# The first stage of a YOCO-style decoder step (S5 layer beside memory keys and values) written as one fixed order of instructions

## The chip, the cores and the metric

One Trainium2 chip, one core. The metric is device time in microseconds (us) of one execution; less is better. The kernel is written in a tile framework: the code names tiles and instructions, the framework adds the semaphores between engines, and its scheduler decides in which order each engine's instructions stand in the program. Once built, each engine runs its own list strictly in that order.

## What is computed

A decoder trunk of two layers over 256 prompt tokens and 64 sample tokens (320 columns, width 1024). Layer 0 mixes with an S5 state space, layer 1 with latent attention; each layer then attends to 256 memory tokens and applies an MLP. The change concerns the S5 part of layer 0 and the keys and values of its memory:

```python
def s5_mixer(u, a_re, a_im, log_dt, b_re, b_im, c_re, c_im, d_skip, w_glu, h0_re, h0_im):
    ...
    _, _, h_re, h_im = lax.associative_scan(
        _complex_affine_combine, (a_seq_re, a_seq_im, bu_re, bu_im), axis=1)
    ...
    y = jnp.einsum('gkn,btgn->btgk', cr, h_re) - jnp.einsum('gkn,btgn->btgk', ci, h_im)
    y = y.reshape(bsz, t, dm) + d_skip.astype(f32) * u.astype(f32)
    g = jax.nn.gelu(y, approximate=False).astype(u.dtype)
    z = g @ w_glu
    out = z[..., :dm] * jax.nn.sigmoid(z[..., dm:])
    return out, h_re[:, -1], h_im[:, -1]

def mem_kv(mem, g, w_k, w_v):
    b, m, _ = mem.shape
    mn = rms_norm(mem, g)
    k = (mn @ w_k).reshape(b, m, MEM_HEADS, MEM_HEAD_DIM)
    v = (mn @ w_v).reshape(b, m, MEM_HEADS, MEM_HEAD_DIM)
    return k, v
```

## The kernel before

Engines are called PE (matmuls and transposes), ACT, DVE, POOL (GpSimd) and SP (which only starts DMAs here). ACT and POOL start DMAs too; a DMA that an engine starts stands in that engine's list.

**The first stage** is `s5_scan` (L711) with the generator `mem_kv` (L575), which makes the memory keys and values. Its parts, by the tiles that name them in the rows:

- Parameters: `an` and `ld` are loaded, turned by PE (`aps`, L768) into `AR`, and become powers PR and PI through exponentials and sines on ACT (L774 to L786) and small products on DVE.
- Memory: `mt` (256 memory tokens) is turned in eight blocks (`mps`) and copied with its gain to `mnp`, four blocks by ACT (L568) and four by DVE (L566). Sixteen chunks of w_mem_k and w_mem_v (512 KB each) are loaded into the weight buffers `wraw`, `whi`, `wlo`, two of each kind, in turn. A chunk gives eight products (`mm`, L600 for keys, L602 for values). Eight groups of two chunks are then written out.
- Tables b and c: `natb` and `natc` are turned in four steps each (`bcps`) and copied to `m_b` and `m_c` (L822).
- x: `xc` holds the tokens by chunk of eight. ACT sums its squares (`sq`, L835), scales it to `xr` (L942), PE turns it (`ups`), ACT copies it to `U` (L950).
- State side, four quarters (hq 0 to 3), `state_side` (L988): DVE makes `tq` from m_b (three products of 128x1024 per half), PE turns it (`rps`), ACT copies it to `rt` (L934), PE multiplies with U (`sps`, L996), ACT copies to `H`.
- Output side, four quarters, `out_side` (L1003): DVE makes `ca` and `ct` from m_c; PE makes the responses (`kps`, L1029, L1033), ACT copies them to `kk` (L1036), DVE adds the skip term (L1042), and eight DMAs on SP spread kk into the Toeplitz tile `tt` (L1045). There is one kk buffer, so a quarter's copies wait until the DMAs of the quarter before have read it.
- `scan` (L1049) runs on DVE twice, over two quarters each, and copies the result to `HS`; `outputs` (L1088) multiplies tt with U and ca, ct with HS on PE (`yps`), turns the result (`ytp`), and ACT applies the GELU and writes `xh`, DVE `xl` (L97, L98).

After that come the GLU products (`glu`, L691, through `dense`, L220): w_glu in sixteen chunks, each loaded by two DMAs into `wraw`, split by ACT into `whi` (L191) and by DVE into `wlo` (L192); three matmuls (L216 to L218) per block. The first group has four chunks and 96 matmuls; two of its chunks need only hq 0 and 1.

**What sets the order.** The scheduler orders each engine's list by its own estimate of times; `tc.issue_after(...)` ties single instructions. GLU loads, conversions and matmuls may so be placed between instructions of the first stage. The two halves of tt are cleared at the start by GpSimd:

```python
        for t in tts:
            nc.gpsimd.memset(t, 0.0)
```

DMAs that SP and ACT start share eight completion slots (DMAHW0 to DMAHW7), handed out in the order in which the code creates the DMAs, over both engines together. Before an engine starts a DMA, its list waits until the last DMA of the same slot has landed.

Of the kernel before, what the change touches and what calls it, by code (L numbers as in the profile page):

```python
# [10 lines left out]
F32 = mybir.dt.float32  # L11
# [74 lines left out]
EARLY = 4  # L86
# [3 lines left out]
class Trunk:  # L90
# [88 lines left out]
    def load_chunk(self, srcs, cols):  # L179

        nc = self.nc
        raw = self.wtile('raw', F32)
# [20 lines left out]
    def plain_tile(self):  # L203
        kind = ('raw', 'hi', 'lo')[self.plain % 3]
        self.plain += 1
        return self.wtile(kind, F32)
# [128 lines left out]
    def build(self):  # L335
        tc, nc, I, O = self.tc, self.nc, self.I, self.O
        with ExitStack() as ctx:
# [11 lines left out]
            self.fillers = []  # L349
# [50 lines left out]
    def mem_gains(self, pool):  # L400
        nc, cp = self.nc, self.cp
        self.gmT = cp.tile([128, 16], F32, name="gmT")
        gn = pool.tile([16, 128], F32, name="gmn")
        nc.scalar.dma_start(gn, self.I['mem_in_norm'].rearrange("l (j p) -> (l j) p", p=128))
        yield
        ps = self.ps_mm.tile([128, 512], F32, name="gps", tag="mm")
        self.transpose(ps[:, :16], gn)
        nc.vector.tensor_copy(self.gmT, ps[:, :16])
        yield

    def load_gains(self, pool):
# [7 lines left out]
        nc.sync.dma_start(gn[106:109, :], I['q_norm'].rearrange("l (j p) -> (l j) p", p=128))  # L419
        ps = self.ps_mm.tile([128, 512], F32, name="gps", tag="mm")  # L420
        self.transpose(ps[:, :109], gn)
        nc.vector.tensor_copy(self.gT[:, :109], ps[:, :109])
# [104 lines left out]
    def mem_x(self, pool, plain=False):  # L527
        if plain:
            return pool.tile([128, KD, MT], F32, name="mnp"), None
        return (pool.tile([128, KD, MT], F32R, name="mnh"), pool.tile([128, KD, MT], F32R, name="mnl"))  # L530
# [7 lines left out]
    def mem_root(self, sq):  # L538

        nc, mt = self.nc, self.mt  # L540
        rm = self.rm = self.cp.tile([128, 2, 2], F32, name="r_mem")
        for i in range(2):
            nc.scalar.activation(sq, mt[i], AF.Square, accum_out=rm[:, 0, i:i + 1])
        yield
        nc.scalar.activation(rm[:, 1], rm[:, 0], AF.Sqrt, bias=self.eps[:, 0:1], scale=1.0 / D)
        nc.vector.reciprocal(rm[:, 0], rm[:, 1])
        yield

    def mem_rows(self):
        nc = self.nc  # L550
        ps = self.ps_mm.tile([128, 512], F32, name="mrb", tag="mm")
        for i in range(2):
            self.transpose(ps[:, i * 128:(i + 1) * 128], self.rm[:, 0, i:i + 1].to_broadcast([128, 128]))
        nc.vector.tensor_copy(self.rB, ps[:, :MT])

    def mem_prepare(self, l, mp, x):
# [3 lines left out]
        for j in range(KD):  # L560
            ps = (self.ps_at if l else self.ps_mm).tile([128, 512], F32, name="mps", tag="at" if l else "mm")
# [3 lines left out]
            if xl is None and j % 2:  # L565
                nc.vector.tensor_scalar(xh[:, j, :], m, g(j), None, op0=ALU.mult)  # L566
            else:
                last = nc.scalar.activation(xh[:, j, :], m, AF.Copy, scale=g(j))  # L568
            if xl is not None:
                nc.vector.scalar_tensor_tensor(xl[:, j, :], m, g(j), xh[:, j, :].bitcast(F32),  # L570
                                               op0=ALU.mult, op1=ALU.subtract)
        self.kt = mp.tile([128, KD, MT], F32, name="kt", tag="kt")
        return last

    def mem_kv(self, l, op, x):  # L575
# [6 lines left out]
        done = {}  # L582

        def products(g):
            W, c0 = (Wk, g * 256) if g < 4 else (Wv, (g - 4) * 256)
            ps = [self.ps_mm.tile([128, 512], F32, name="mm", tag="mm") for _ in range(2)]
            for k0 in range(0, KD, 4):
                src = W[:, k0:k0 + 4, c0:c0 + 256]
                if xl is None:
                    raw = self.ahead.pop(0) if self.ahead else self.load_plain(src)  # L590
                    with ExitStack() as after:
                        if self.mem_hold is not None:
                            after.enter_context(self.tc.issue_after(self.mem_hold.ins))
                        for kk in range(4):
                            k = k0 + kk
                            for b in range(2):
                                w = raw[:, kk * 256:(kk + 1) * 256]
                                bs = slice(b * 128, (b + 1) * 128)
                                if g < 4:
                                    last = nc.tensor.matmul(ps[b][:, :MT], w[:, bs], xh[:, k, :], start=k == 0, stop=k == KD - 1)  # L600
                                else:
                                    last = nc.tensor.matmul(ps[b][:, :256], xh[:, k, bs], w, start=k == 0, stop=k == KD - 1)  # L602
                    if g < EARLY and k0 == 0:
                        yield last
                    continue
                hi, lo = self.load_chunk([(lambda t: t.rearrange("p (k c) -> p k c", c=256), src)], 1024)
                for kk in range(4):
                    k = k0 + kk
                    for b in range(2):
# [3 lines left out]
                        else:  # L613
                            s = slice(kk * 256, (kk + 1) * 256)
                            ms = slice(b * 128, (b + 1) * 128)
                            self.mm3(ps[b][:, :256], xh[:, k, ms], xl[:, k, ms], hi[:, s], lo[:, s], k == 0, k == KD - 1)
            if g < 4:
                for b in range(2):
                    nc.scalar.activation(kt[:, 2 * g + b, :], ps[b][:, :MT], AF.Copy)
            done[g] = ps  # L620
            if not l and g < EARLY:
                yield last

        if not l:
            for g in range(EARLY):
                yield from products(g)
# [1279 lines left out]
```

## Time and profile before

| what | us |
|---|---|
| median of 3 runs | 1213.37 |
| runs | 1212.70, 1213.37, 1215.11 |
| the profiled execution, own time | 1214.59 |
| its span, first to last instruction | 1212.9 |
| PE busy in the span | 1134.4 (94%) |
| DVE, ACT, POOL busy | 701.8, 558.1, 54.2 |

The rows read from the trace stand further down. In a timeline row the first number is the start in us from the span's start, the second the time from the first start to the last end, `xN` the number of instruction records (a product has two records, a transpose one), and the bracket the idle time ahead of it with what ended it. A row of DMA on SPq or ACTq is the starting of the DMA, not its transfer.

### The profile page before, as it was taken

How to read it: one execution, taken by the hardware profiler on the slowest of the kernel's cores; microseconds unless marked ns; L12 is line 12 of the kernel's file. 1: busy time of each engine (PE TensorE's matmuls, PEld its weight loads, DVE VectorE, ACT ScalarE, POOL GpSimd, SP SyncE). 2: the span in 40 equal slices, each digit the busy share in tenths (PEclk: the TensorE clock that was granted, in tenths of full speed). 3: DMA queues.
4: the chain of work that ended last, by engine and by line, in shares of the span. 5: the costliest groups of instructions: out<-in, count | busy, mean ns of one | idle time of the engine just before them, and what ended most of it. 6: DMA issues, size and time to landing. Idle time of an engine off the chain costs nothing.

```text
span 1212.9 us, 21264 instructions
## 1 busy us (share of the span) xinstructions
PE 1134.4 (94%) x8233; PEld 1027.4 (85%) x8233; DVE 701.8 (58%) x1344; ACT 558.1 (46%) x1012; POOL 54.2 (4%) x91
## 2 busy tenths in 40 slices
PE   5799789899899999999999999999998999999995
PEld 4688679886699999999988984579966899999995
DVE  6697834674369643564686674417842675335553
ACT  5664554444355543553464362224443465334531
POOL 1000000000000000000000154100000000000001
PEclk9799899999899999999999999989999999999998
DMA  9346358747244544444453555447470434444541
GB/s 179 98 132 153 81 130 290 261 154 262 88 123 132 170 154 147 148 156 144 159 149 109 154 178 157 141 146 283 147 269 25 138 122 141 156 139 144 167 142 44
DMA packets 155233, 185.37 MB, mean 153 GB/s; under 512 B 20847, under 2 KB 123516, under 8 KB 155068
## 3 DMA queue, kind: packets, MB, share of 16 engines
q1 hardware_dynamic: 145660, 175.36, 47.0%
q10 hardware_dynamic: 7008, 5.47, 1.4%
q0 software_dynamic: 2464, 3.19, 0.9%
q8 instruction: 65, 1.06, 0.4%
q14 instruction: 36, 0.29, 0.1%
HBM read 175.41 MB, written 6.21 MB: 150 GB/s over the span
## 4 chain that ended last, share of the span: by engine, by line
PE 75%; ACT 3%; DVE 3%; issue 1%; DMA 0%; POOLq 0%; POOL 0%; ACTq 0%; DVEq 0%
PE mm L217 19%; PE mm L216 19%; PE mm L218 19%; PE kt L103 2%; PE sps L1282 2%; PE s L1765 2%; PE ops L1297 1%; ACT whi L191 1%; PE pov L1339 1%; PE s L1806 1%; PE ltp L103 1%; DVE wlo L192 1%; PE pps L1317 1%; PE turn L103 1%; PE s L1768 1%
## 5 line engine op out<-in xcount | busy, mean ns | idle before, releaser
L192 DVE TENSOR_TENSOR wlo<-wraw,whi 128x1024 fp32r<-128x1024 f32 (+1 forms) x216 | 259.6, 1205 | 280.4 <-ACT whi L191 262.2
L191 ACT ACTIVATE whi<-wraw 128x1024 fp32r<-128x1024 f32 (+1 forms) x216 | 224.6, 1045 | 304.8 <-PE mm L217 253.3
L217 PE MATMUL mm<-xl,whi 128*128 128x320 f32 x944 | 292.8, 313 | 1.6 <-DVE xl L293 0.9
L216 PE MATMUL mm<-xh,whi 128*128 128x320 f32 x944 | 278.9, 316 | 15.7 <-ACT whi L191 4.6
L218 PE MATMUL mm<-xh,wlo 128*128 128x320 f32 x944 | 282.2, 312 | 0.0
L216 PEld LDWEIGHTS mm<-xh,whi 128*128 128x128 f32 x944 | 174.9, 191 | 19.6 <-ACT xh L1309 5.0
L217 PEld LDWEIGHTS mm<-xl,whi 128*128 128x128 f32 x944 | 179.7, 190 | 3.2 <-DVE xl L293 1.7
L218 PEld LDWEIGHTS mm<-xh,wlo 128*128 128x128 f32 x944 | 176.9, 190 | 0.2 <-DVE wlo L192 0.2
L216 PE MATMUL mm<-hh,whi 128*128 128x320 f32 x512 | 158.0, 309 | 0.0
L217 PE MATMUL mm<-hl,whi 128*128 128x320 f32 x512 | 158.0, 309 | 0.0
L218 PE MATMUL mm<-hh,wlo 128*128 128x320 f32 x512 | 157.1, 308 | 0.0
L217 PEld LDWEIGHTS mm<-hl,whi 128*128 128x128 f32 x512 | 96.1, 188 | 0.0
L216 PEld LDWEIGHTS mm<-hh,whi 128*128 128x128 f32 x512 | 96.1, 188 | 0.0
L218 PEld LDWEIGHTS mm<-hh,wlo 128*128 128x128 f32 x512 | 95.9, 188 | 0.0
L103 PE MATMUL kt<-ident,kn 128*128 128x128 f32 x256 | 37.1, 280 | 5.2 <-ACT ktb L1209 2.8
L103 PEld LDWEIGHTS kt<-ident,kn 128*128 128x128 f32 x256 | 27.9, 141 | 16.5 <-DVE ktb L1207 5.2
L1694 POOL DMA_DIRECT2D rop<-in_cache_k_rope x64 | 35.0, 547 | 37.1 <-issue 10.5
L119 DVE TENSOR_TENSOR sq<-sq 128x320 f32<-128x320 f32 x67 | 32.2, 481 | 2.1 <-ACT sq L121 1.3
L1398 DVE TENSOR_TENSOR t_up<-t_up 128x320 f32<-128x320 f32 x64 | 29.8, 486 | 2.0 <-ACT hh L1397 1.9
L1399 DVE TENSOR_TENSOR hl<-t_up,hh 128x320 fp32r<-128x320 f32 x64 | 29.8, 487 | 0.9
L1207 DVE COPY ktb<-kt 128x512 f32<-128x512 f32 x32 | 22.0, 687 | 13.2 <-PE kt L103 12.7
L1397 ACT ACTIVATE hh<-t_up 128x320 fp32r<-128x320 f32 x64 | 28.4, 472 | 0.9
(486 smaller groups left out, 1797.3 us busy)
## 6 DMA issues: line engine op xcount, KB each, us to landing
wraw<-in_w_mlp_up SPq DMA_DIRECT2D x64, 512.0 KB, 3.7
wraw<-in_w_mlp_down SPq DMA_DIRECT2D x64, 512.0 KB, 3.4
kn<-in_cache_mem_k SPq DMA_DIRECT2D x16, 1024.0 KB, 4.9
vn<-in_cache_mem_v SPq DMA_DIRECT2D x16, 1024.0 KB, 7.8
wraw<-in_w_glu SPq DMA_DIRECT2D x32, 256.0 KB, 3.0
wraw<-in_w_mem_q SPq DMA_DIRECT2D x16, 512.0 KB, 6.0
wraw<-in_w_mem_o SPq DMA_DIRECT2D x16, 512.0 KB, 3.6
lat<-in_cache_kv_latent SPq DMA_DIRECT2D x64, 128.0 KB, 2.7
```

The source lines that it names most:

```text
L103: return self.nc.tensor.transpose(out, in_, self.ident[b:b + k, b:b + k])
L119: eng.tensor_add(st['acc'], st['acc'], st['last'])
L191: nc.scalar.activation(hi[:, :cols], raw[:, :cols], AF.Copy)
L192: nc.vector.tensor_sub(lo[:, :cols], raw[:, :cols], hi[:, :cols].bitcast(F32))
L216: nc.tensor.matmul(ps, wh, xh, start=start, stop=False)
L217: nc.tensor.matmul(ps, wh, xl, start=False, stop=False)
L218: nc.tensor.matmul(ps, wl, xh, start=False, stop=stop)
L1282: nc.tensor.matmul(sps[h * 32:(h + 1) * 32, :MT], qm[:, h * 2 + db, j * 128 + i * 32:j * 128 + (i + 1) * 32], ktb[:, h * 2 + db, :], start ...
L1397: A.activation(hh[b // 4][:, b % 4, :], a, AF.Square)
L1398: V.tensor_mul(a, a, a)
L1399: V.tensor_sub(hl[b // 4][:, b % 4, :], a, hh[b // 4][:, b % 4, :].bitcast(F32))
L1694: last[eng] = eng.dma_start(dst, src[bass.ds(v, 1)].rearrange("o p d -> (o p) d"))
```

## The change

`s5_scan` is written again as one sequence. A new context `in_order` goes over everything that is created in it and ties, on PE, DVE, ACT and SP, each instruction to the one before it on its engine, so that the order of the code is the order of the list. POOL is not tied.

- The loads of x and of c move from SP to ACT's list, behind the first gain copy (`load_x`). The memory chunks use four buffers (`raw`, `hi`) in place of six.
- The sixteen chunks of products are placed one by one between the steps of the state work.
- tt is cleared by a DVE memset and an ACT copy; the copy of `ld` goes from DVE to ACT; the skip term's products and adds (L1116, L1117 of the new file) and the starts of the key and value stores go to POOL.
- The first GLU chunk is created inside the sequence (`glu_chunk`), behind the gains (`gn`), which are now loaded after the last tt. The final states are turned after the sequence's outputs.
- kk keeps one buffer; ca and ct get more.

```diff
+    def in_order(self, engines):
+
+        @contextmanager
+        def block():
+            traced = self.nc.cur_bb.bb.instructions
+            first = len(traced)
+            yield
+            last = {}
+            for i in traced[first:]:
+                if i.engine in engines:
+                    if i.engine in last:
+                        self.tc.add_manual_dep(i, last[i.engine].name, mybir.DependencyInfo(
+                            mybir.DependencyClass.NoSync, mybir.DependencyReason.DATA), reason="in_order")
+                    last[i.engine] = i
+        return block()
...
-        close_s8 = self.s5_scan(sp, mkv, mx)
...
+        with self.in_order((mybir.EngineType.PE, mybir.EngineType.DVE, mybir.EngineType.Activation, mybir.EngineType.SP)):
+            close_s8 = self.s5_scan(sp, mkv, mn)
...
+        def load_x():
+            for i in range(2):
+                cols = slice(i * D // 2, (i + 1) * D // 2)
+                A.dma_start(xc[i * NCH:i * NCH + NC_P], I['x_prompt'][0].rearrange("(c s) d -> c s d", s=L)[:, :, cols])
+                A.dma_start(xc[i * NCH + NC_P:(i + 1) * NCH], I['x_sample'][:, :, cols])
+            for i, part in enumerate(('re', 'im')):
+                for o in range(2):
+                    A.dma_start(nat['c'][i * G:(i + 1) * G, :, o], I[f'ssm_c_{part}'][0])
...
+        V.memset(tts[0], 0.0)
...
+        mem_block(0)
+        load_x()
+        mem_block(1)
+        A.activation(w(6), w(5), AF.Sin)
+        A.activation(w(7), w(5), AF.Sin, scale=0.5)
...
+        A.activation(tts[1].rearrange("p s u k -> p (s u k)"), tts[0].rearrange("p s u k -> p (s u k)"), AF.Copy)
+        products(0)
+        products(1)
...
-        for t in tts:
-            nc.gpsimd.memset(t, 0.0)
...
+        responses(3)
+        responses_out(3)
+        scan(1)
+        products(14)
+        products(15)
+        gn = self.load_gains(sp)
+        scanned(1)
+        outputs_low(0)
+        outputs_low(1)
+        outputs(2, 0)
+        self.chunks_ahead = [self.glu_chunk(0)]
+        values_out(7)
+        outputs(2, 1)
+        outputs(3, 0)
+        outputs_turned(2)
+        outputs_high(2)
+        outputs(3, 1)
...
```

In the lists below, `[waits DMAHWn...]` is a wait for the slot's last DMA, and `xc`, `natc` are the loads of x and c.

ACT's list at the start, before: the sines (L785) and the four gain copies (L568) follow each other.

```order
L777 ACTIVATE W<-eps 128x1
L774 ACT_TABLE_LOAD
L774 ACTIVATE W<-AR 128x64 [waits DVE_49]
L776 ACTIVATE W<-W 128x64 [waits DVE_49]
L785 ACT_TABLE_LOAD
L785 ACTIVATE W<-W 128x64 [waits DVE_49]
L786 ACTIVATE W<-W 128x64
L568 ACTIVATE mnp<-mps,gmT 128x256 [waits PE_49] x4
```

The same place now; slots 5 to 7 and 0 to 4 were last given to mt, mt, w_mem_k chunk 0, bn, bn and w_mem_k chunks 1, 2 and 3.

```order
L794 ACTIVATE mnp<-mps,gmT 128x256 [waits PE_49]
L701 DMA xc<-in_x_prompt 32x8x512 [waits DMAHW5_49]
L702 DMA xc<-in_x_sample 8x8x512 [waits DMAHW6_49]
L701 DMA xc<-in_x_prompt 32x8x512 [waits DMAHW7_49]
L702 DMA xc<-in_x_sample 8x8x512 [waits DMAHW0_49]
L705 DMA natc<-in_ssm_c_re 64x16x64 [waits DMAHW1_49]
L705 DMA natc<-in_ssm_c_re 64x16x64 [waits DMAHW2_49]
L705 DMA natc<-in_ssm_c_im 64x16x64 [waits DMAHW3_49]
L705 DMA natc<-in_ssm_c_im 64x16x64 [waits DMAHW4_49]
L836 ACTIVATE W<-W 128x64 [waits DVE_49]
L837 ACTIVATE W<-W 128x64
L794 ACTIVATE mnp<-mps,gmT 128x256 [waits PE_49] x3
```

Eight starts of DMAs, each with a slot wait, the last three for chunks 1 to 3, now stand ahead of the sines and of three gain copies on ACT.

SP's list at the end of the stage, before: ten w_glu loads ahead of the third quarter's tt, two more behind it.

```order
L184 DMA wraw<-in_w_glu 128x2x256 x10
L1045 DMA tt<-kk 16x2048
...
L1045 DMA tt<-kk 16x256
L184 DMA wraw<-in_w_glu 128x2x256 x2
```

The same place now: the last DMA of the last quarter's tt, the nine gain loads, then the first w_glu load.

```order
L1120 DMA tt<-kk 16x256
L406 DMA gn<-in_norm_mix_pre 16x128
L406 DMA gn<-in_norm_mix_post 16x128
L406 DMA gn<-in_norm_mem_pre 16x128
L406 DMA gn<-in_norm_mem_post 16x128
L406 DMA gn<-in_norm_mlp_pre 16x128
L406 DMA gn<-in_norm_mlp_post 16x128
L407 DMA gn<-in_kv_in_norm 8x128
L408 DMA gn<-in_kv_latent_norm 2x128
L409 DMA gn<-in_q_norm 3x128
L185 DMA wraw<-in_w_glu 128x2x256 x10
```

No w_glu load is started any more before all four quarters of tt and the gains.

PE's list, now, where the GLU begins (before, GLU matmuls stood between the last three quarters' outputs):

```order
L102 MATMUL ytp<-ident,yc 128x128 x8
L102 MATMUL gps<-ident,gn 128x109
L217 MATMUL mm<-xh,whi 128x320
L218 MATMUL mm<-xl,whi 128x320
L219 MATMUL mm<-xh,wlo 128x320
```

All GLU matmuls stand behind the last turning of the outputs.

## Rows read from the trace of the kernel before

**Rows 1.** Busy time by stretch of the span: engines, PEclk, DMA share, GB/s.
```profile
0.00:76.70 76.70, 56.03 (x282) 47.54 (x282) 54.68 (x123) 49.43 (x104) 6.03 (x10) 0.89 0.56 134
180.20:245.00 64.80, 59.74 (x413) 57.55 (x412) 36.31 (x57) 31.53 (x51) 0.51 (x1) 1.00 0.76 266
```

**Rows 2.** Timeline of PE: the first three chunks of products.
```profile
12.91 5.64 PE L600 MATMUL mm<-mnp,wraw 128*128 128x256 f32 x16
18.39 3.62 PE L600 MATMUL mm<-mnp,whi 128*128 128x256 f32 x16
...
29.09 6.08 PE L600 MATMUL mm<-mnp,wlo 128*128 128x256 f32 x16 [6.21 <-DMA wlo<-in_w_mem_k]
```

**Rows 3.** Busy time by stretch, the first 33 us: columns as in rows 1.
```profile
0.00:9.00 9.00, 2.05 (x8) 1.36 (x8) 5.44 (x15) 4.80 (x8) 6.03 (x10) 1.00 0.62 201
9.00:15.00 6.00, 5.07 (x18) 4.04 (x18) 4.06 (x17) 5.11 (x10) 0.00 (x0) 1.00 1.09 208
15.00:24.00 9.00, 7.88 (x36) 6.56 (x35) 7.87 (x30) 3.04 (x5) 0.00 (x0) 1.00 1.09 167
24.00:33.00 9.00, 3.90 (x9) 3.20 (x10) 4.87 (x16) 7.18 (x20) 0.00 (x0) 0.67 0.92 165
```

**Rows 4.** Timeline of SP's DMA starts: c's third load.
```profile
19.86 8.02 SPq L761 DMA_DIRECT2D natc<-in_ssm_c_im  x1
```

**Rows 5.** Timeline of ACT: copies of the state work.
```profile
33.01 0.63 ACT L835 ACTIVATE sq<-xc 80x512 f32<-80x512 f32 x1
33.55 0.19 ACT L835 ACTIVATION_READ_ACCUMULATOR sq<-xc 80x1 f32 x1
35.65 1.91 ACT L822 ACTIVATE m_b<-bcps 128x512 f32<-128x512 f32 x2 [1.91 <-PE bcps L103]
...
44.81 5.01 ACT L942 ACTIVATE xr<-xc,rC 80x512 f32<-80x512 f32 x8 [1.24 <-DVE rC L841]
...
59.78 1.09 ACT L934 ACTIVATE rt<-rps 128x512 f32<-128x512 f32 x2
...
68.41 0.76 ACT L950 ACTIVATE U<-ups 128x320 f32<-128x320 f32 x2
```

**Rows 6.** Timeline of PE: one quarter's states, responses, turning; outputs.
```profile
79.27 2.06 PE L996 MATMUL sps<-U,rt 128*64 128x40 f32 x64
...
118.99 0.44 PE L1100 MATMUL yps<-tt,U 128*64 128x128 f32 x4
...
124.38 1.99 PE L602 MATMUL mm<-whi,mnp 128*128 128x256 f32 x8
126.22 1.08 PE L103 MATMUL ytp<-ident,yc 128*128 128x128 f32 x8
...
143.69 1.07 PE L1029 MATMUL kps<-ca,bz 128*16 128x128 f32 x32
```

**Rows 7.** Timeline of ACT: the kk copies of the first two quarters.
```profile
87.61 2.42 ACT L1036 ACTIVATE kk<-kps 16x512 f32<-16x512 f32 x4 [1.30 <-PE kps L1033]
...
100.05 2.41 ACT L1036 ACTIVATE kk<-kps 16x512 f32<-16x512 f32 x4 [3.25 <-DMA tt<-kk]
```

**Rows 8.** Timeline of POOL: the clearing of the two halves of tt.
```profile
3.66 3.57 POOL L902 MEMSET tt<- 128x2048 f32 x2
```

**Rows 9.** Timeline of SP: gains (first and last of nine), w_glu, last tt.
```profile
47.58 0.34 SPq L416 DMA_DIRECT2D gn<-in_norm_mix_pre  x1
...
50.95 0.25 SPq L419 DMA_DIRECT2D gn<-in_q_norm  x1
...
110.52 28.41 SPq L184 DMA_DIRECT2D wraw<-in_w_glu  x10
...
154.87 6.09 SPq L1045 DMA_DIRECT2D tt<-kk  x8
```

**Rows 10.** DMA issues of the page: engine, op, count, KB each, median us to landing.
```profile
wraw<-in_w_glu SPq DMA_DIRECT2D x32, 256.0 KB, 3.0
```

**Rows 11.** Timeline of PE: the second group of the GLU begins.
```profile
180.20 0.31 PE L216 MATMUL mm<-xh,whi 128*128 128x320 f32 x1
```

More of the change, by code (lines that the diff above doesn't have):

```diff
@@ L588, in products @@
                 src = W[:, k0:k0 + 4, c0:c0 + 256]
[L589 to L605, printed above, removed]
                 hi, lo = self.load_chunk([(lambda t: t.rearrange("p (k c) -> p k c", c=256), src)], 1024)
@@ new lines, in s5_scan, with products @@
+        load(1)
+        load(2)
+        load(3)
+        ps_of = {}
+        kt = self.kt = mkv.tile([128, KD, MT], F32, name="kt", tag="kt")
+        def products(i, between=None):
+            g, k0 = i // 2, i % 2 * 4
+            if k0 == 0:
+                ps_of[g] = [mm("mm"), mm("mm")]
+            raw = raws.pop(i)
+            for kk in range(4):
+                if kk == 2 and between is not None:
+                    between()
+                k = k0 + kk
+                for b in range(2):
+                    w = raw[:, kk * 256:(kk + 1) * 256]
+                    bs = slice(b * 128, (b + 1) * 128)
+                    o = ps_of[g][b][:, :256]
+                    if g < 4:
+                        nc.tensor.matmul(o, w[:, bs], mnp[:, k, :], start=k == 0, stop=k == KD - 1)
+                    else:
+                        nc.tensor.matmul(o, mnp[:, k, bs], w, start=k == 0, stop=k == KD - 1)
+            load(i + 4)
@@ new lines, in s5_scan @@
+        out_weights(0, 0)
+        out_weights(0, 1)
+        states(0)
+        states(1)
+        long_powers()
+        V.memset(H[:, :, :, 0], 0.0)
+        out_weights(1, 0)
+        products(7)
+        keys(3)
+        keys_out(0)
+        initial_states()
+        out_weights(1, 1)
+        responses(0)
+        responses_out(0)
+        products(8)
+        scan(0)
+        responses(1)
+        responses_out(1)
+        keys_turned(1)
+        products(9)
+        values_out(4)
+        keys_out(1)
@@ new lines, in s5_scan @@
+        keys_turned(2)
+        products(10)
+        scanned(0)
+        outputs(0, 0)
+        outputs(0, 1)
+        state_weights(2, 0)
+        state_turned(2, 0)
+        keys_out(2)
+        keys_turned(3)
+        state_weights(2, 1)
+        state_turned(2, 1)
+        products(11)
+        keys_out(3)
+        values_out(5)
+        states(2)
+        state_weights(3, 0)
+        state_turned(3, 0)
+        outputs(1, 0)
+        outputs(1, 1)
+        state_weights(3, 1)
+        state_turned(3, 1)
@@ new lines, in s5_scan @@
+        states(3)
+        outputs_turned(0)
+        outputs_high(0)
+        out_weights(2, 0)
+        out_weights(2, 1)
+        products(12)
+        responses(2)
+        responses_out(2)
+        outputs_turned(1)
+        outputs_high(1)
+        out_weights(3, 0)
+        out_weights(3, 1)
+        products(13)
+        values_out(6)
+        responses(3)
[5 more added lines that the diff above has]
+        scanned(1)
```

703 lines of the change are left out of this document (364 added, 339 removed).

## The prediction

> **What bounds the kernel now.** I read the busy time by stretch first. PE is busy for 94% of the span, but in the first 76.7 us for only 56.03 us; in the stretch after 180.2 us it is busy for 59.74 of 64.8 [rows 1]. The change touches the stage ahead of 180.2, where the second group of the GLU begins on PE; nothing behind that point is rewritten. So the measure is one number: when does that group begin afterwards?
>
> The timeline of PE comes next. The first chunk of products starts at 12.91, the second at 18.39, the third only at 29.09, after 6.21 us of waiting for w_mem_k [rows 2]. The early idle time is supply, and the stretches say why: from 9 to 24 us the DMA share is 1.09, with 208 and 167 GB/s moved; it is 0.92 with 165 GB/s from 24 to 33 [rows 3]. There is no slack in the transfers that an earlier start could use.
>
> Then SP: the third load of c took 8.02 us to start, because its list was held for a completion slot [rows 4]. SP only starts DMAs, so that stop delayed later loads, but no arithmetic.
>
> **The part that I think decides: ACT is held.** Now x and c are started by ACT, and the eight starts stand ahead of the sines and three of its gain copies. By the list, their slots were last given to mt, mt, chunk 0, bn, bn, and chunks 1, 2 and 3. ACT goes on when chunk 3 has landed; I call that time F. No row of before shows ACT held like this, so I bound F.
>
> Bytes: small loads 0.15 MB, mt 1.05, four chunks 2.10, bn 0.52, x 1.31, together 5.13 MB (0.52 is a chunk of 512 KB, the rest from shapes). The stretches move 201 x 9 = 1.81 MB by 9 us, 1.25 more by 15, 1.50 more by 24 and 165 GB/s from there [rows 3]. 5.13 MB are reached at 27.5 us. With the first two loads of c (0.52 MB, started ahead of the end) it is 30.6. I take 29, between the two. Low end: if the weights land as if x were not there, 3.82 MB are reached at 19.5, and chunk 0 (behind 0.15, 1.05 and 0.52 MB, reached at 8.6) was used at 12.91 [rows 2], about 4 later: 23.5. High end: 30.6 and 4, so 34.6. If the slots were free at once there would be a pure issue cost: ACT reaches the starts some 2 us before PE used the gain copies at 12.91 [rows 2], and eight starts at 0.7 each (between a gain's 0.34 and a tt's 0.76 [rows 9]) make F = 16.5.
>
> The Trainium skill has a rule that speaks against this part: "DMA: Bandwidth & Descriptors", section "Issuing engines are not separate DMA queues", says that DMAs started by different engines share the same 16 DMA engines and interleave, and that starting on several saves only the starting engine's time. The trace agrees so far: the share is already at 1.09 [rows 3]. By the rule F is 29 and the forecast below stands; with x free beside the weights F is 23.5 and the time is 1215.5.
>
> **The chain from F to the GLU.** After that each engine goes strictly by the code, so I add the steps, following the engine that releases the next one.
>
> (a) F to the last copy of m_b: five small ACT instructions, taken like U's copies at 0.38 each with a gap [rows 5], 2.2; three chunks of products, 5.64, 3.62 and 3.6 [rows 2]; two turnings of 1.0, as ytp [rows 6]; a copy of 0.95 [rows 5]. 18.0.
>
> (b) ACT without a gap: eight squares at 0.63 and 0.19, 6.6; four m_c copies at 0.95, 3.8; xr 5.0; eight rt copies at 0.55, 4.4; eight U copies at 0.38, 3.0 [rows 5]; two key copies, a root with its table load, bz and the small tables, which have no row here and are taken as six of m_b's size, 6.0. 28.8.
>
> (c) PE: states of two quarters 4.1 and a turning 1.1; one chunk 3.6 [rows 2]; responses 2.1, twice 1.07 [rows 6]; then the kk copies 2.4 [rows 7]. 13.3.
>
> (d) One kk buffer is kept: the second quarter's copies start at 100.05, 10.0 after the first ended at 90.03, and ACT waited there on the DMAs that read kk [rows 7]. The gap stays: 10.0, the copies 2.4, and the value copies 0.8 (two of U's size), which free PSUM for the next chunk on PE. 13.2.
>
> (e) PE in a row: three chunks 10.6; outputs of two quarters, 118.99 to 124.38 less its gap, 5.3 each, 10.6; turnings of tq, keys and yc, 5.2; states of two quarters 4.1; half a response 1.05 [rows 6]. 31.5.
>
> (f) Copies of kk for the third and the fourth quarter, 2.4, 10.0 and 2.4 [rows 7], and the skip add, now on GpSimd. No row shows a GpSimd add: its clearing took 3.57 for two memsets of 128x2048 [rows 8], 1.8 for one. The add is on 16 partitions, so I take 0.9, with ends 0 and 1.8. 15.7.
>
> (g) SP: eight starts of the last tt 6.1; nine gain loads, 47.58 to 51.20, 3.6; the two starts of the first w_glu chunk, some 1.0 by the gains' spacing [rows 9]; landing 3.0 [rows 10]. 13.7. Before, ten w_glu starts stood at 110.52 to 138.9, ahead of the third quarter's tt, and hid all this [rows 9].
>
> (h) ACT: eleven instructions (two splits of w_glu, yc, GELU, xh, values) between U's 0.38 and m_b's 0.95 [rows 5], at 0.75. 8.3.
>
> Together 142.5, so the first GLU matmul comes at 29 + 142.5 = 171.5. Behind it stands the whole first group, 96 matmuls at 0.145 (59.74 / 413 [rows 1]), 13.9, and the turnings of the final states with their copies, 2.4. Before, many of these matmuls filled gaps between outputs. The second group then begins at 187.8, against 180.20 [rows 11]: **7.6 us later**.
>
> Costed at nothing: the clearing that leaves GpSimd, and the log_dt copy that leaves DVE, since what they speed up (parameters) waits at the held ACT. If F falls under 21.4 they begin to count, by 2 us at most. The first GLU loads reach ACT a little after the output copies do; if they came at once, the outputs would be next. Four chunk buffers in place of six: the chunks are consumed slower than the 3.4 us that PE needs each, so their loads hide. The stores on GpSimd have nobody waiting.
>
> The profiled execution took 1214.59, with 1.7 outside its span, and is 1.2 over the median of 1213.37. The difference of 7.6 is made against that execution and laid on the median: **1221.0**. About 0.2%, 2.4 us, is what a measurement can tell from no change.
>
> **The rivals.**
>
> *ACT isn't held to chunk 3, faster.* If the slots are free when ACT arrives, F is 16.5, the chain ends at 159.0 and the second group begins at 175.3: 4.9 earlier, 1208.5. The products then run between the state work without PE's 6.21 us of waiting [rows 2]. It decides below F = 21.4. For it: mt has landed by then, and two of eight slots are free at once. Against it: a start on SP was held for 8.02 by just such a wait [rows 4], and chunk 2 was not there before 29 [rows 2]. 0.23.
>
> *Weights land first, x behind, about the same.* F = 23.5, the second group at 182.3, 2.1 later, 1215.5. For it: the weights' starts stand in time ahead of x's. Against it: the DMA engines are full [rows 3], and mixed loads share. 0.14.
>
> *The GLU's weights become the bound, slower still.* All their loads start only at (g), where before ten were started by 138.9 [rows 9]. If each further chunk of the first group needs its own starts, landing and split, 0.9 + 3.0 [rows 10] + 1.0, before its matmuls, 4.9 for each of three chunks, 14.7 in all, comes on top if nothing hides it; the matmuls of the chunk before hide about half: 7.4 more, 1228.4. For it: no load stands ahead any more. Against it: the ten starts stand in one go, so transfers overlap. 0.15.
>
> That the sequence is not kept is no case of its own: the tie binds the lists, and the lists show it.
>
> **How the numbers follow.** Forecast 0.48 (F from 27.5 to 34.6 and the add's ends give 1218.6 to 1227.5). The faster rival has 0.23, and of the forecast's case 0.03 more falls there, since the chain counts small steps by neighbours: faster 0.26, same 0.14, slower 0.45 + 0.15 = 0.60. The range reaches from just under the faster rival to just over the slowest, 1207 to 1230; within the slower cases its own range is 1217 to 1230.
>
> **What would show it.** Right: ACT idle from about 11 to about 29 us ahead of an x or c start or the sines, put down to w_mem_k's DMA; PE's first chunk of products at about 31 and the states at about 75; the kk copies of quarters two and four again waiting on tt's DMAs; w_glu's first start at about 157, behind the gains; the first GLU matmul at about 171 and the second group at about 188. Wrong: a first chunk of products before 23, which means that ACT was not held, or GLU matmuls well before 165 after a late first chunk, which means that the chain from F is shorter than 142.5. If the first GLU group itself takes over 20 us, the third rival is true.

## The result and the profile after

The changed kernel is slower than before, and by more than was forecast. Its four runs took 1227.92, 1231.64, 1231.92 and 1231.91 us (median 1231.78); the kernel before took 1213.03 beside them. The ratio is 1.0147, 95% interval 1.0120 to 1.0173, so 14.6 to 21.0 us. A second set of runs gave 1.0137 (1.0112 to 1.0161), with medians of 1226.64 after and 1212.36 before. The forecast was 1221.0 with a range to 1230.

| what | before, us | after, us |
|---|---|---|
| the profiled execution, own time | 1214.59 | 1227.92 |
| its span | 1212.9 | 1226.3 |
| PE busy in the span | 1134.4 (94%) | 1131.8 (92%) |
| first chunk of products starts on PE | 12.91 [rows 2] | 28.88 |
| second group of the GLU starts on PE | 180.20 [rows 11] | 192.18 |

Busy time by stretch of the changed kernel (columns as in [rows 1]; the stretches that answer to [rows 1], and three short ones with a low granted clock):

```profile
0.00:76.70 76.70, 48.00 (x363) 41.20 (x363) 44.35 (x110) 44.28 (x94) 6.26 (x14) 0.87 0.52 133
...
192.20:257.00 64.80, 59.64 (x406) 56.86 (x407) 34.60 (x55) 29.91 (x51) 0.00 (x0) 1.00 0.77 266
...
15.00:24.00 9.00, 0.00 (x0) 0.00 (x0) 0.00 (x0) 0.00 (x0) 0.00 (x0) 0.53 1.12 190
...
98.70:105.20 6.50, 6.47 (x18) 5.01 (x20) 6.34 (x10) 2.99 (x7) 2.74 (x4) 0.57 0.69 115
...
169.00:172.00 3.00, 2.87 (x18) 2.54 (x20) 1.62 (x3) 2.69 (x7) 0.00 (x0) 0.50 0.59 209
```

Behind the second group's start PE is as busy as before (59.64 of 64.8 against 59.74). In the first 76.7 us it does 8 us less than before, and from 15 to 24 us nothing runs on any engine but the transfers. ACT's timeline says why. A row of ACTq is the start of a DMA; a wait for a slot is not in the row, it is the gap ahead of it. So the second start of c begins at 14.10, when chunk 1, whose slot it waits for, has landed, 8.4 us after its start at 5.69 (the starts of c are shown one by one):

```profile
9.17 0.47 ACT L794 ACTIVATE mnp<-mps,gmT 128x256 f32<-128x256 f32 x1 [1.10 <-PE mps L102]
9.18 0.69 ACTq L701 DMA_DIRECT2D xc<-in_x_prompt  x1
...
13.10 0.58 ACTq L705 DMA_DIRECT2D natc<-in_ssm_c_re  x1
14.10 4.54 ACTq L705 DMA_DIRECT2D natc<-in_ssm_c_re  x1
18.69 7.76 ACTq L705 DMA_DIRECT2D natc<-in_ssm_c_im  x1
26.98 0.56 ACTq L705 DMA_DIRECT2D natc<-in_ssm_c_im  x1
27.58 0.26 ACT L836 ACTIVATE W<-W 128x64 f32<-128x64 f32 x1 [17.93 <-DMA natc<-in_ssm_c_re]
...
27.89 1.19 ACT L794 ACTIVATE mnp<-mps,gmT 128x256 f32<-128x256 f32 x3
```

The four starts of x pass in some 3.5 us, those of c take 14.4 us. Only some 1.0 of these are gaps, the last one ahead of 26.98; the second and the third start are themselves 4.54 and 7.76 long. The sines and three gain copies stand behind them and come at 27.58. PE's timeline, at the points that the prediction named:

```profile
28.40 0.69 PE L102 MATMUL mps<-ident,mt 128*128 128x128 f32 x2 [16.70 <-ACT mnp L794]
28.88 5.50 PE L742 MATMUL mm<-mnp,wraw 128*128 128x256 f32 x16
...
72.92 4.05 PE L1049 MATMUL sps<-U,rt 128*64 128x40 f32 x128 [0.20 <-ACT U L990]
...
98.73 6.47 PE L744 MATMUL mm<-wraw,mnp 128*128 128x256 f32 x16 [5.28 <-ACT wlo L782]
...
169.13 1.97 PE L102 MATMUL ytp<-ident,yg 128*128 128x128 f32 x8 [6.76 <-ACT yg L1190]
...
175.40 0.39 PE L217 MATMUL mm<-xh,whi 128*128 128x320 f32 x1
...
192.18 0.42 PE L217 MATMUL mm<-xh,whi 128*128 128x320 f32 x1 [0.48 <-ACT t_up L647]
```

PE's four longest waits until 192 us, from the view of waits:

```profile
PE mps L102 <- ACT mnp L794: 16.7, 1, 16.7
PE ytp L102 <- ACT yg L1190: 6.8, 1, 6.8
PE yps L1189 <- DVE HS L1160: 6.4, 1, 6.4
PE mm L744 <- ACT wlo L782: 5.3, 1, 5.3
```

The first is the held ACT. The second is in the tail. There ACT's list has splits of w_glu between the copies of the outputs, and they wait for weights whose loads start only behind the last tt and the gains, at 161.07 on SP:

```profile
158.81 0.60 ACT L1190 ACTIVATE yg<-yps 128x512 f32<-128x512 f32 x1 [3.40 <-PE yps L1189]
164.62 1.06 ACT L192 ACTIVATE whi<-wraw 128x1024 fp32r<-128x1024 f32 x1 [5.22 <-DMA wraw<-in_w_glu]
...
167.54 1.06 ACT L192 ACTIVATE whi<-wraw 128x1024 fp32r<-128x1024 f32 x1 [1.13 <-DMA wraw<-in_w_glu]
168.50 0.58 ACT L1190 ACTIVATE yg<-yps 128x512 f32<-128x512 f32 x1
```

Three theories were formed from this. H: the hold of ACT is the loss, and the stage carries it to its end. T: the tail loses by itself, through w_glu's loads or splits. S: the second scan on DVE, for which PE waits 6.4 us, sets the tail. Against H stood that the states begin at 72.92, earlier than before, as if the hold were made up by then (PE's timeline of the kernel before):

```profile
76.73 2.06 PE L996 MATMUL sps<-U,rt 128*64 128x40 f32 x64
```

### The profile page after: what moved, and what is told of

The parts are those of the page before. It is cut to its first block, busy times and chain, and to the rows that moved or that the text cites. A ratio compares the mean times of both kernels' runs of the same rounds, so it can differ in the third digit from the quotient of the medians.

```text
span 1226.3 us, 21300 instructions
## 1 busy us (share of the span) xinstructions
PE 1131.8 (92%) x8233; PEld 1025.4 (84%) x8233; DVE 701.9 (57%) x1327; ACT 555.9 (45%) x1012; POOL 65.8 (5%) x110
## 3 DMA queue, kind: packets, MB, share of 16 engines
HBM read 175.41 MB, written 6.21 MB: 148 GB/s over the span
## 4 chain that ended last, share of the span: by engine, by line
PE 82%; ACT 6%; DVE 6%; DMA 3%; issue 1%; SPq 1%; POOL 0%; POOLq 0%; ACTq 0%; DVEq 0%
PE mm L218 19%; PE mm L217 19%; PE mm L219 19%; PE mm L742 2%; PE kt L102 2%; PE sps L1451 2%; PE s L1934 2%; ACT whi L192 2%; PE ops L1466 1%; PE pov L1508 1%; PE s L1975 1%; DMA natc<-in_ssm_c_re 1%; DVE wlo L193 1%; PE ltp L102 1%; PE pps L1486 1%
## 5 line engine op out<-in xcount | busy, mean ns | idle before, releaser
L192 ACT ACTIVATE whi<-wraw 128x1024 fp32r<-128x1024 f32 (+1 forms) x216 | 224.4, 1045 | 309.4 <-PE mm L218 252.1
```

The source lines that it names most:

```text
L192: nc.scalar.activation(hi[:, :cols], raw[:, :cols], AF.Copy)
```

## The experiments

Whole times of one kernel spread by 1 to 13 us from run to run. So each experiment is read by two numbers: the ratio of its runs to runs of the kernel before on the same chip, and in its profile the place of the first summing of squares behind the GLU (tile `ss`), the first landmark behind the stage that all kernels share. Not every small difference there is an effect: the states of the four tied kernels with x and c on SP and DVE's clearing, whose code is the same up to there, start between 53.83 and 56.53. For the kernel before and for the two profiles of the changed kernel (line, engine, operation, count: ns of one, first and last start):

```profile
L129 PE MATMUL ss<-sq,ones x2: 432/432/433, 227.9 to 228.2; 128*128 128x320 f32 x2
```

```profile
L128 PE MATMUL ss<-sq,ones x2: 432/432/432, 240.6 to 240.9; 128*128 128x320 f32 x2
```

```profile
L128 PE MATMUL ss<-sq,ones x2: 432/432/432, 239.9 to 240.2; 128*128 128x320 f32 x2
```

| kernel | first squares, us | ratio to before, 95% interval |
|---|---|---|
| before | 227.9 | 1 |
| the change | 240.6 | 1.0147 (1.0120 to 1.0173) |
| the change, second profile | 239.9 | 1.0137 (1.0112 to 1.0161) |
| x and c started by SP | 224.6 | 0.9971 (0.9948 to 0.9994) |
| c alone started by SP | 239.5 | 1.0108 (1.0074 to 1.0142) |
| before, x and c started by ACT | 236.8 | 1.0057 (1.0030 to 1.0084) |
| x and c by SP, nothing tied | 224.3 | 0.9975 (0.9947 to 1.0003) |
| x and c by SP, GpSimd clears | 225.0 | 1.0005 (0.9987 to 1.0023) |
| first w_glu chunk and gains ahead | 240.9 | 1.0092 (1.0058 to 1.0127) |
| order on DVE | 241.5 | 1.0136 (1.0113 to 1.0159) |
| splits behind the outputs | 236.7 | 1.0068 (1.0034 to 1.0103) |
| x and c, weights, DVE together | 222.9 | 0.9939 (0.9917 to 0.9962) |
| these and the splits | 217.2 | 0.9903 (0.9867 to 0.9939) |
| and the value copies | 215.6 | 0.9918 (0.9890 to 0.9946) |

### The starts of x and c

All eight loads go to SP, in the same place of the program:

```diff
-                A.dma_start(xc[i * NCH:i * NCH + NC_P], ...
+                nc.sync.dma_start(xc[i * NCH:i * NCH + NC_P], ...
...
-                    A.dma_start(nat['c'][i * G:(i + 1) * G, :, o], ...
+                    nc.sync.dma_start(nat['c'][i * G:(i + 1) * G, :, o], ...
```

> The eight loads of x and c are started by SP behind chunk 3's, in place of ACT; nothing else changes. Theory H (the held ACT is the loss, and it is carried to the end of the stage): the first chunk of products starts at about 13 to 15 us in place of 28.9, the states at 62 to 66 in place of 72.9, and the whole is 8 to 11 us faster than the changed kernel (about 1221 to 1224 where that has 1231.8; ratio to before about 1.006 to 1.009). Rival M (made up): since the states of the changed kernel come earlier than before's (72.9 against 76.73), the hold is paid back before them; then less than 2 us is won, and the ratio stays at 1.013 or more.

H, and more of it than expected at every point. ACT's sines come at 9.57 in place of 27.58, and PE follows (timelines of ACT and of PE of this kernel):

```profile
9.57 0.25 ACT L836 ACTIVATE W<-W 128x64 f32<-128x64 f32 x1
```

```profile
11.94 4.42 PE L742 MATMUL mm<-mnp,wraw 128*128 128x256 f32 x16
...
53.83 2.36 PE L1049 MATMUL sps<-U,rt 128*64 128x40 f32 x70 [0.20 <-ACT U L990]
...
159.60 0.39 PE L217 MATMUL mm<-xh,whi 128*128 128x320 f32 x1
```

The first chunk is 16.9 us earlier, the states 19.1, the first GLU matmul 15.8, the first squares 16.0. The ratio falls from 1.0147 to 0.9971, by 21 us on 1213. I had expected 8 to 11. The hold is not made up before the states. The states of the changed kernel come early in spite of it, since its sequence puts them ahead of products: seven chunks stand before them on PE, nine in the kernel before.

SP is now the engine that is held: its starts of c last until 27.13, as ACT's did until 27.54, and of the arithmetic only PE waits behind it, once, 2.20 us for c itself. What holds SP is not a slot, though. Its last two starts of c wait for the slots of chunks 2 and 3, and chunk 3 landed 10.1 us after its start at 6.97, at 17.1 (view of chunk 3's load). The third start alone lasts until 26.12:

```profile
15.84 10.28 SPq L705 DMA_DIRECT2D natc<-in_ssm_c_im  x1
```

```profile
DMA to landing us min/median/max: 10.1/10.1/10.1
```

In the changed kernel chunk 3 landed 20.1 us after its start at 6.88, at 27.0, just when ACT's fourth start of c begins (26.98):

```profile
DMA to landing us min/median/max: 20.1/20.1/20.1
```

So ACT was held in two ways that end together there: the third start lasts until 26.45 by itself, and the slot of chunk 3 comes free at 27.0. What makes some starts of c long (0.56 to 10.28 us for loads of the same shape), no run shows.

Between 9 and 24 us the DMA share is 1.08 to 1.12 in both kernels, and chunk 3 lands 10 us later where x and c are started by ACT beside it than where they stand behind it on SP. This agrees with the Trainium skill ("DMA: Bandwidth & Descriptors", "Issuing engines are not separate DMA queues"): DMAs of different engines run on the same 16 DMA engines and interleave.

Next, only c's four loads go to SP:

```diff
-                    A.dma_start(nat['c'][i * G:(i + 1) * G, :, o], ...
+                    nc.sync.dma_start(nat['c'][i * G:(i + 1) * G, :, o], ...
```

> Of the eight loads only the four of c go to SP; the four of x stay with ACT, in their place. Their slots were last given to mt, mt, chunk 0 and the first bn load, c's to bn and chunks 1 to 3. Theory H (ACT is held by the slots of chunks 1 to 3, that is by c's starts alone): ACT goes on at about 12 to 14 us in place of 27.6, the first chunk of products comes at 13 to 16, and the time is within 4 us of the kernel with all eight on SP (ratio to before 0.995 to 1.002). Rival B (the transfers of x hold things up, whoever starts them, or any start on ACT costs): the first chunk of products after 20, ratio over 1.006.

These are B's numbers: the first chunk starts at 23.74, the ratio is 1.0108. The list shows where my reasoning for H failed. Slots are handed out over both engines in the order of the finished program, not in the order in which the code creates the loads, as is said ahead of the prediction. There c's starts on SP stand between x's on ACT, so x's four starts now wait for slots 6, 0, 2 and 4 in place of 5, 6, 7 and 0. Slot 4 belongs to chunk 3. ACT's timeline:

```profile
21.68 0.71 ACTq L702 DMA_DIRECT2D xc<-in_x_sample  x1
22.44 0.26 ACT L836 ACTIVATE W<-W 128x64 f32<-128x64 f32 x1 [12.77 <-DMA whi<-in_w_mem_k]
```

ACT's third start of x ends at 14.58, and the fourth comes 7.1 us later: x's starts alone hold ACT here, as B has it, but by a slot, and not by x's transfers. The middle dose is of use: 5.1 us less hold brought 5.1 us at the first chunk, 4.6 at the states, 3.6 at the fourth quarter's kk copies (143.73 for 147.32) and 4.7 us by the ratio (0.0039 of 1213), but only 1.1 at the squares. Most of the loss between (2.5 of 4.0) lies in the tail, where a third split of w_glu stands ahead of the second copy of yg; the changed kernel has two there, and that copy comes at 168.50, only 1.5 later:

```profile
165.99 1.06 ACT L192 ACTIVATE whi<-wraw 128x1024 fp32r<-128x1024 f32 x1 [0.39 <-DMA wraw<-in_w_glu]
166.96 0.58 ACT L1190 ACTIVATE yg<-yps 128x512 f32<-128x512 f32 x1
```

The kernel with all eight starts on SP has the same third split there: its fourth kk copies come 18.2 earlier than the change's, that copy of yg 15.9.

The part alone, in the kernel before:

```diff
-            nc.sync.dma_start(xc[i * NCH:i * NCH + NC_P], ...
+            nc.scalar.dma_start(xc[i * NCH:i * NCH + NC_P], ...
...
-                nc.sync.dma_start(nat['c'][i * G:(i + 1) * G, :, o], ...
+                nc.scalar.dma_start(nat['c'][i * G:(i + 1) * G, :, o], ...
```

> The kernel before with one part of the change alone: the eight loads of x and c are started by ACT. The scheduler puts them at the head of ACT's list, ahead of its first arithmetic, with slot waits for loads that end early as well as for chunks. Theory H: ACT is held there too, until the last slot that c's starts wait for has landed (about 15 to 28 us), the first chunk of products comes that much later than 12.91, and as the stage follows one to one the kernel is 4 to 16 us slower than before (ratio 1.003 to 1.013). Rival: the sequence, not the starts, made the hold; then the time is that of before within 2 us.

H again, but not one to one: PE's first chunk comes at 28.78, 15.9 us later, the states come 9.2 and the squares 8.9 later; by the ratio it is 0.0057, 6.9 us. The scheduler had put the starts at the head of ACT's list, and ACT does no arithmetic until 24.73:

```profile
16.49 8.20 ACTq L761 DMA_DIRECT2D natc<-in_ssm_c_im  x2
24.73 1.28 ACT L773 ACT_TABLE_LOAD   x1 [24.73 <-DMA natc<-in_ssm_c_re]
```

By the list the slots of c's starts belonged to the loads of x here, not to chunks, and the last 8.2 us are two starts of c, 3.34 and 4.82 long. So the hold needs neither the sequence nor its ties, nor a chunk's slot. The ties were taken out by themselves, with x and c on SP:

```diff
-        with self.in_order((mybir.EngineType.PE, mybir.EngineType.DVE, ...
-            close_s8 = self.s5_scan(sp, mkv, mn)
+        close_s8 = self.s5_scan(sp, mkv, mn)
```

> x and c on SP, and no instruction tied to the one before it: the scheduler orders every engine again. It tells what the ties are worth by themselves. Theory O (the fixed order keeps the state work in front and is where the gain of the kernel with x on SP comes from): 3 us or more slower than that kernel, ratio over 0.9995. Theory N (the ties cost, since GLU loads, splits and matmuls can no longer stand between): 3 us or more faster, ratio under 0.9946.

Neither: 224.3 against 224.6 at the squares, 0.9975 against 0.9971. The ties by themselves are worth nothing that can be told here, though the stage runs otherwise without them: the states begin at 71.16 in place of 53.83, the first GLU matmul at 128.31 in place of 159.60.

### The clearing

```diff
-        V.memset(tts[0], 0.0)
+        for t in tts:
+            PQ.memset(t, 0.0)
...
-        A.activation(tts[1]..., tts[0]..., AF.Copy)
```

> The kernel with x and c on SP, and tt cleared by two memsets on GpSimd as before, in place of a DVE memset and an ACT copy of 1.9 us. Theory C (GpSimd's clearing slows DVE at the start, as the 4.11 us copy of before suggests, and the parameters come later): the first sine and the gain copies come 2 us later and the time is 1 to 2 us longer than with x on SP alone. Rival: ACT and DVE are not late at that point and save their 1.9 and 1.8 us; then no difference over 1 us, or slightly faster. Either is near the limit of what can be told; the traces decide.

One of DVE's small operations, which takes 0.20 without, took 0.70 beside GpSimd's 3.56 us of memsets; no other in this stretch is so much longer:

```profile
6.58 0.70 DVE L827 TENSOR_SCALAR W<-W 128x64 f32<-128x64 f32 x1
7.31 0.25 DVE L828 TENSOR_SCALAR W<-W 128x64 f32<-128x64 f32 x1
```

The sines and gain copies did not come later (9.51 against 9.57), and the squares are 0.4 us later. Theory C falls in the trace. The ratio of 1.0005 beside 0.9971, from other runs on another chip, is more than the stage shows; whether any of it is the clearing's stays open.

### The tail

The loads of the first GLU chunk and the gains go ahead of the last tt, the splits stay:

```diff
         values_out(6)
+        raw = self.glu_raw(0)
+        gn = self.load_gains(sp)
         responses(3)
...
-        gn = self.load_gains(sp)
...
-        self.chunks_ahead = [self.glu_chunk(0)]
+        self.chunks_ahead = [self.glu_split(raw)]
```

> The loads of the first GLU chunk and of the gains are started before the last quarter's tt, the splits stay where they are. Theory T (the tail: ACT stands at w_glu's split from 159.4 to 164.6 with the output copies behind it, and that wait goes straight to the first GLU matmul): the split no longer waits, the turning of yg starts at about 163 to 164 in place of 169.1, the first GLU matmul at about 170 in place of 175.4, 5 to 6 us faster than the changed kernel, ratio about 1.010. Rival S (the second scan, which ends at 155, holds the outputs on PE until 162.4 whatever the weights do): less than 2 us won.

The first squares stayed (240.9), as S has it, but not for S's reason. The split of another chunk, which is created behind the sequence and not tied, was put by the scheduler ahead of the copies of yg, and waited there for its own load:

```profile
164.76 1.06 ACT L192 ACTIVATE whi<-wraw 128x1024 fp32r<-128x1024 f32 x1 [8.66 <-DMA wraw<-in_w_glu]
165.84 0.60 ACT L1201 ACTIVATE yg<-yps 128x512 f32<-128x512 f32 x1
166.33 1.05 ACT L632 ACTIVATE whi<-wraw 128x1024 fp32r<-128x1024 f32 x1
```

L632 is the split of the first chunk, which no longer waits, L192 the one that slipped ahead. The ratio of 1.0092 lies below the change's, but the stage gives no cause for it.

The order on DVE alone:

```diff
         state_turned(2, 1)
+        out_weights(2, 0)
         products(11)
...
         state_turned(3, 0)
+        out_weights(2, 1)
         outputs(1, 0)
...
-        out_weights(2, 0)
-        out_weights(2, 1)
         products(12)
```

> The output weights of the third quarter are made on DVE between the state weights, where DVE sat idle for 3.4 and 4.7 us waiting for tq buffers; the same instructions, only their order. Theory S (the second scan's end sets the tail): the scan ends at about 147 in place of 154.1, PE no longer waits 6.4 us for HS, and 5 to 7 us are won, ratio about 1.010. Theory T: the scan does end at about 147, but ACT still waits for w_glu until about 164.6, and the first GLU matmul stays within 1 us of 175.4: less than 1.5 us won.

T's side. PE's wait for HS falls from 6.4 to 2.2 us, and ACT's for w_glu grows from 5.2 to 9.0; nothing is won. The first GLU matmul even comes at 177.65, 2.3 us later, for here too a third split stands ahead of the second copy of yg (timelines of PE and of ACT):

```profile
151.03 0.43 PE L1189 MATMUL yps<-hca,HS 128*64 128x128 f32 x2 [2.15 <-ACT HS L1159]
```

```profile
164.60 1.06 ACT L192 ACTIVATE whi<-wraw 128x1024 fp32r<-128x1024 f32 x1 [8.97 <-DMA wraw<-in_w_glu]
```

Then the splits of the first four chunks behind the last output copy, loads as they were:

```diff
-        self.chunks_ahead = [self.glu_chunk(0)]
+        raw = self.glu_raw(0)
...
-        outputs(3, 1)
+        last = outputs(3, 1)
+        self.chunks_ahead = [self.glu_split(raw)]
+        self.hold = {self.chunk + i: last for i in (1, 2, 3)}
```

> The changed kernel with ACT's splits of the first four GLU chunks placed behind the last output copy; the loads start where they did. Theory T2 (in the kernel with the weights ahead, the wait stayed because the scheduler put the second chunk's split, which is not part of the sequence, ahead of the output copies; it is the splits' place in ACT's list that costs, not only the loads): the copies of yg follow PE at 159 to 163, the turning of yg starts by 164 in place of 169.1, the first GLU matmul at 169 to 171 in place of 175.4, and the time falls by 4 to 6 us against the changed kernel (ratio about 1.010). Rival L (the weights land at 164.6 to 169 and are the bound themselves): the first GLU matmul stays at 173 or later, less than 2 us won.

T2. ACT no longer stands still between the copies:

```profile
159.09 0.60 ACT L1201 ACTIVATE yg<-yps 128x512 f32<-128x512 f32 x1 [3.40 <-PE yps L1200]
...
160.96 0.60 ACT L1201 ACTIVATE yg<-yps 128x512 f32<-128x512 f32 x1 [0.40 <-PE yps L1200]
...
166.33 1.06 ACT L632 ACTIVATE whi<-wraw 128x1024 fp32r<-128x1024 f32 x1
```

The first GLU matmul comes at 167.44 (8.0 earlier), the second group at 185.49 (6.7 earlier), the squares at 236.7 (3.9 earlier; PE's clock is 0.97 in that stretch, 1.00 in the changed kernel's). The ratio falls by 0.007 to 0.008.

### Together

The three first edits of SP, weights and DVE in one kernel:

> The three edits together. If H, T and S are three losses in a row: 8 to 11 by the start, 5 to 6 by the weights and 5 to 7 more once the weights are there, in all some 18 to 24 us faster than the changed kernel, 1208 to 1214, the same as before or a little faster. If M holds: 1219 to 1223. If something else than these three bounds the stage: over 1223.

The squares come at 222.9, 17.7 earlier than in the change, of which 16.0 are H's; by the ratio it is 25 us, so the 18 to 24 expected lie between the two measures. ACT's wait ahead of yg is 11.6 us there, again for a split that slipped ahead. With the splits behind the outputs as well:

> The kernel with x and c on SP, the weights and gains ahead, the order on DVE, and the splits behind the last output copy. T2: ACT's wait of 11.6 us for w_glu ahead of yg goes; the first GLU matmul comes 6 to 9 us earlier than in the three together, ratio to before 0.987 to 0.990. Rival L: PE then waits for the splits or the weights itself, less than 3 us won, ratio 0.992 or more.

The squares come at 217.2, 5.7 earlier, and by the ratio 4.4 us are won: nearer to T2 than to L, at its low end. One edit more puts the value copies ahead of the second quarter's kk copies:

```diff
         responses(1)
-        responses_out(1)
         keys_turned(1)
         products(9)
         values_out(4)
         keys_out(1)
+        responses_out(1)
```

> The four edits and one more: the value copies that free PSUM for the tenth chunk stand ahead of the second quarter's kk copies on ACT, which wait for tt's DMAs. PE's wait of 5.25 us ahead of that chunk, and the slow clock behind it (the chunk took about 6.1 to 6.5 us where others take 3.6), should go, some 7 us of PE. Theory P (PE's row of work is the bound there, as the prediction's terms d and e had it): 4 to 7 us faster than the four together, ratio 0.985 to 0.987. Rival V (DVE, which works there without a gap, is the bound): the chunk comes earlier, but the second scan ends at the same time, less than 2 us won.

V by its number: at the squares 1.6 us are won. The chunk that waited comes at 76.85 and takes 3.64 us (82.32 with the four edits), but DVE's last copy for the second scan, ending at 129.74 in place of 131.73, is only 2 us earlier. That DVE is the bound isn't shown by this alone: part of the gain went into a new wait of PE, 3.03 us for the first scan's HS, which ACT copies behind the second quarter's kk copies. The timelines of PE and of DVE:

```profile
76.85 3.64 PE L755 MATMUL mm<-wraw,mnp 128*128 128x256 f32 x16
...
83.89 1.14 PE L1200 MATMUL yps<-ca,HS 128*64 128x128 f32 x3 [3.03 <-ACT HS L1170]
```

```profile
129.32 0.42 DVE L1173 COPY HS<-H 64x512 f32<-64x512 f32 x1
```

The ratios of the two last kernels, 0.9903 and 0.9918, can't be told apart; they are some 10 to 12 us faster than before and some 29 us faster than the change.

Last, the changed kernel once more:

> The changed kernel as it is, for a second profile and more runs: its profiled run took 1227.92 and its other three 1231.6 to 1231.9. If the stage itself varies, the second profile shows the first summing of squares behind the GLU at another place than 240.6 us; if only later stages do, it stays within 1 us of 240.6. Ratio to before 1.012 to 1.017.

The squares repeat within 0.7 us. The span was 1219.7 against 1226.3, so 5.9 of those 6.6 us came behind the squares. From there to the end the kernel before takes 985.0 us, the two profiles of the change 985.7 and 979.8, and all others 981.8 to 989.9, in no order that the edits would explain.

## Why the prediction was wrong

That ACT is held and that the stage carries the delay to its end was right. The sum was too small, by terms e and h, and the first set's median lies 1.8 us above the range (the second set's inside it).

**The held ACT: right.** Forecast was that ACT goes on at F = 29, between 27.5 and 34.6; it went on at 27.58, the low end of the bytes' bracket, after chunk 3 had landed at 27.0. The first chunk of products was to come at about 31 and came at 28.88. The reason was seen in part, and here the sum had luck. The 8.02 of [rows 4] is, read as above, the length of a start and no wait for a slot, and a start was priced at 0.7, where c's second and third took 4.54 and 7.76. Without any slot wait the eight rows alone, 16.7 us from 9.18, would have held ACT until about 26 (an estimate from these rows), near enough to F.

**Terms a to d: right, 2.1 us too long.** From F to the tenth chunk on PE 73.3 were forecast, and 71.15 passed (27.58 to 98.73). The kk buffer's gap, priced at 10.0, is there (kk's copies end at 86.01 and start again at 95.78).

**Term e: the step that failed first.** 31.5 was forecast for PE's row from that chunk to the third quarter's kk copies; it took 36.1 (98.73 to 134.87). The chunk alone took 6.47 where [rows 2] gave 3.6. PE had waited 5.28 us for the value copies, and the granted clock behind that wait was 0.57, mostly at the lower of its two levels, 1.2 GHz. The prediction priced the wait and not what came behind it, although the chunk that followed a wait of 6.21 in the kernel before took 6.08 [rows 2]. The rest, 1.7, is spread over turnings (5.9 with the waits between them, for 5.2), the response (1.46 for 1.05), states and outputs. That the kernel pays for such a chunk in full isn't shown: with the four edits, where the weights' loads no longer hang on this row, taking the wait and the slow chunk away brought the next kk copies 3.2 us forward (118.86 to 115.70) and the squares 1.6.

**Terms f and g: right.** 15.7 and 13.7 were forecast, 15.8 and 13.95 came (134.87, 150.67, 164.62). The GpSimd add took 0.81 to 1.47, for 0.9.

**Term h: too small by 2.5.** 8.3 was forecast from the first split to the first GLU matmul, and 10.8 passed (164.62 to 175.40). I had eleven ACT instructions in a row. The path was another: ACT, which waits 1.13 for a second chunk, sets it only until 169.13, then PE. After 6.76 us of waiting PE turns yg at a clock of 0.50 in 1.97 us, where 1.08 is its time [rows 6], multiplies the last half of the outputs until 173.74, and turns them once more behind ACT's copy. These steps of PE have no place in the term.

**The GLU's first group: 16.8 for 16.3.** So the second group starts at 27.58 + 71.15 + 36.1 + 15.8 + 13.95 + 10.8 + 16.8 = 192.18, where 187.8 was forecast: 12.0 us behind before, not 7.6.

**What lies behind the stage: open.** The squares are 12.0 to 12.7 us late in two profiles; the medians of the two sets lie 18.8 and 14.3 apart. Of the 10.8 us between the forecast and the first median, 4.4 are the stage's, by the terms above; the other 6.4 are not explained. The prediction laid the stage's difference on the whole, and what is behind the squares differs by 10 us between profiles in no order that the edits would explain. Whether the change adds a few us there, these runs don't settle.

**The rivals.** That ACT isn't held was wrong. Its price, 4.9 us faster, is near the 3.3 at the squares and 3.5 by the ratio of the kernel without the hold, but partly by luck: there ACT goes on at 9.57, not at 16.5, and from there to the first GLU matmul 150.0 us pass, not 142.5. That the weights land ahead of x is true of that kernel (chunk 3 at 17.1), not of the change, where ACT went on at 27.58 and not at 23.5. The GLU's weights as a bound were wrong by the prediction's own sign, a first group of over 20 us: it took 16.8. Their late loads were in the sum (g), and an extra price lay in the splits' place on ACT, as the kernel with late splits shows (3.9 at the squares).

**Costed at nothing: right by the squares** for the clearing (0.4 us where ACT is not held); the ratio leaves it open.

## What to carry to other kernels

A DMA start that stands in the list of an arithmetic engine can hold that engine twice: by its slot's wait, the gap ahead of its row (7.1 us for x in the kernel with c on SP), and by its own length (7.76 us for c in the change). So print for each start which earlier DMA its slot belonged to, read the length of the start's row, and put starts that may be held on an engine that only starts DMAs. Slots go round over all starting engines, so moving some starts changes the waits of the others. And where instructions outside a fixed sequence can be scheduled into it, one that waits for a transfer can take the place of the one that was moved away.

## What was not expected

- Two waits of PE, of 5.3 and 6.8 us, had a second price: the granted clock was 0.57 and 0.50 in the stretches behind them, and the chunk behind the first took 2.9 us longer.
- With all eight starts moved, the hold passed to the end of the stage almost one to one (18.0 us at the sines, 16.0 at the squares) over some 200 us, though the states came earlier than before. In this stage earlier states are no sign that a delay has been made up. It is no rule: 5.1 us less hold left 1.1 with c alone on SP, and 15.9 at the first chunk left 8.9 in the kernel before.
- In two profiles of one kernel the landmark behind the stage repeated within 0.7 us, where whole times of a kernel differ by up to 13.
